# Tree attention on one core: TensorE one pair ahead at first, V copied in halves, loads reordered

## The chip, the core and the metric

The kernel runs on one core of a Trainium2 chip. A core has five engines with a queue of instructions each: TensorE (PE; its weight loads are listed as PEld), VectorE (DVE), ScalarE (ACT), GpSimd (POOL) and SyncE (SP), and 16 DMA engines that move data between the device's memory (HBM) and the core's SBUF. An engine works through its queue in order and waits where the next instruction waits. The metric is the device time of one execution in microseconds.

## The reference

Attention over 8 x 12 = 96 heads of 512 positions and 64 dimensions, in which position i may see only itself and its ancestors in a binary tree (the parent of i is (i-1)//2):

```python
    scores = np.einsum('bhqd,bhkd->bhqk', Q, K) * scale
    scores = scores + (1 - mask) * (-1e9)

    weights = np.exp(scores - np.max(scores, axis=-1, keepdims=True))
    weights = weights / (np.sum(weights, axis=-1, keepdims=True) + 1e-10)

    return np.einsum('bhqk,bhkd->bhqd', weights, V).astype(np.float32)
```

Inputs and output are float32.

## The kernel before

The 512 positions of a head lie in SBUF as 128 partitions of 4 "slots". Two heads make a pair; there are 48 pairs (`NP`), and 8 heads (four pairs) make a group (`GB`, 12 groups). The loop variable `i` of the main loop counts pairs. Pair i does the following:

- `transpose(i)` (L250): 16 small TensorE transpositions turn the pair's K and Q into keys and queries with the dimension on partitions. They land in the PSUM tile `kqp`, of which there is one. `evac(i)` (L276, VectorE) copies it to SBUF as `kq`.
- `scores1(i)` and `scores2(i)` (L287 to L325): matmuls that first add mask codes and then the products of keys and queries. The tree is split into an upper part that all queries see (scores1) and a lower part that is restricted to a few key blocks per query (scores2). ScalarE takes the exponential of each (L298, L321), into `e1` and `e2`.
- `values(i)` (L347): 20 matmuls of the exponentials with V, into the PSUM tile `ob`, of which there is one. A column of ones beside V gives the sums of the weights.
- `norm(i)` (L376, L377, VectorE): reciprocal of the sums and the multiplication, into `of`.

V doesn't arrive in the order in which `values` reads it. For each group it is copied from the load tile `vst` into the tile `vt`, in ten copies that all stand at L209: four "l7" copies (`spread_l7`, 32 partitions, VectorE), four "top" copies (`spread_top`, 32 partitions, mostly GpSimd) and two "leaf" copies (`spread_leaves`, 64 partitions, ScalarE or GpSimd). A whole group gives shapes of 32x1024, 32x512 and 64x1024; half a group (4 heads) gives 32x512, 32x256 and 64x512. `vt` has two buffers of two groups each. `spread(i)` says which copies are issued in iteration i. For i below 12 a table (`early_copies`) lists them; from 12 on it is a quarter of group i//4+1 in each iteration: an l7 copy, and on GpSimd two top copies or one leaf copy. Where an iteration has copies on both engines, `after()` makes the first GpSimd copy wait for the last VectorE copy.

All loads but those of the first pair, and all stores, are issued from GpSimd's queue (L189, L385), so they stand in one order with GpSimd's copies. Loads turn float32 into bf16 on the way. Each of K, Q and V has four load tiles of a group each. `loads_at(i)` says which loads are issued in iteration i: the start issues heads 0 to 15 in pieces of 4 heads, and from head 16 on each load is a whole group (8 heads). Stores begin in iteration 33, one group in each iteration; the last group is stored in three pieces.

The whole order on each engine is the order in which these functions are called (`manual_schedule`). In the main loop iteration i calls scores1(i), scores2(i), values(i-1), norm(i-1), transpose(i+2), evac(i+2), spread(i) and the loads or stores of i. Only iterations 1 to 3 differ, by this table:

```python
    AHEAD = {1: (2, 3), 2: (), 3: (4, 5)}
```

`fill(i, n)` issues n matmuls of zeros at the start, while there is no data.

Of the kernel before, what the change touches and what calls it, by code (L numbers as in the profile page):

```python
# [98 lines left out]
def kernel(  # L99
# [12 lines left out]
    NH = B * H  # L112
    NP = NH // 2
# [100 lines left out]
    def spread_top(eng, j, g, h0=0, h1=GB):  # L214
        return copy(
            eng, vtile(g)[32 * j:32 * j + 32, h0:h1, 0, 0:D],
            vsts[g][0:32, h0:h1, UNITS[TOP + j][1], :],
        )

    def spread_leaves(eng, r, g, h0=0, h1=GB):  # L220

        p = 64 if r else 0
        return copy(
            eng, vtile(g)[p:p + 64, h0:h1, 1 + r:4 + r:2, 0:D],
            vsts[g][64:128, h0:h1, r:3 + r:2, :],
        )
# [27 lines left out]
    def transpose(i):  # L254
        kqp = psT.tile([P, 2, 32, 32], bf16, name="kqp")
        kqps[i] = kqp
        for t in range(4):
            for a in range(2):
                transpose_one(kqp[:, 0, :, :], i, a, t, _slot_layout(t)[1], ksts, perms[t])
        for x, t in enumerate(ORDER):  # L260
            for a in range(2):
                transpose_one(
                    kqp[:, 1, :, :], i, a, t, [2 * x, 2 * x + 1, 2 * x + 9, 2 * x + 10],
                    qsts, qperm,
                )

    def evac(i):
        kq = work.tile([P, 2, 16, 32], bf16, name="kq")
        kTs[i] = kq[:, 0, :, :]
        qTs[i] = kq[:, 1, :, :].rearrange("p (t u) c -> p t (u c)", t=4)  # L270
        src = kqps[i][:, :, 0:18, :]
        src = bass.AP(
            src.tensor, src.offset,
            [list(src.ap[0]), [1024, 2], [32, 8], [9 * 32, 2], [1, 32]],
        )
        nc.vector.tensor_copy(  # L276
            out=kq[:, :, :, :].rearrange("p k (x y) c -> p k x y c", y=2), in_=src
        )
# [48 lines left out]
    def fill(i, n):  # L327

        if i not in obs:
            obs[i] = psO.tile([P, 2, 512], fp32, name="ob")  # L330
        for k in range(n):
            nc.tensor.matmul(
                out=obs[i][:, k % 2, :], lhsT=zeros[:, 0:128], rhs=zeros[:, :],
                start=True, stop=True,
            )

    def values(i):

        if i == NP - 1:
            obs[i] = psT.tile([P, 2, 512], fp32, name="kqp")  # L340
        elif i not in obs:
            obs[i] = psO.tile([P, 2, 512], fp32, name="ob")
        ob = obs[i]
        e1, e2, vt = ets[i], e2s[i % NE], vtile(2 * i // GB)

        def product(e, a, t, tile_v, lo=0, hi=128, **flags):
            nc.tensor.matmul(  # L347
                out=ob[lo:hi, a, 65 * t:65 * t + 65],
                lhsT=e[:, a, PLACE[t], lo:hi],
                rhs=vt[:, 2 * i % GB + a, tile_v, 0:D + 1],  # L350
                **flags,
            )

        def first(a):
            for t in range(4):
                product(e1, a, t, 0, start=t == 0, stop=False)
            for t in (2, 3):
                product(e2, a, t, 1 + t, start=False, stop=False)

        def second(a):  # L360
            for t in (0, 1):
                product(e2, a, t, 1 + SELF[t], 0, 64, start=False, stop=t == 1)
                product(e2, a, t, 1 + t, 64, 128, start=False, stop=t == 1)

        order = (first, second) * 2 if i == NP - 1 else (first, first, second, second)
        for n, part in enumerate(order):
            part(n // 2 if i == NP - 1 else n % 2)

    def norm(i, heads=((0, 2),)):
        g, r = divmod(i, 4)  # L370
        if r == 0:
            ofs[g] = opool.tile([P, GB, 4, D], fp32, name="of")
        for a0, a1 in heads:
            o4 = obs[i][:, a0:a1, 0:260].rearrange("p a (t c) -> p a t c", c=D + 1)
            rec = small.tile([P, a1 - a0, 4, 1], fp32, name="rec")
            nc.vector.reciprocal(out=rec[:, :, :, :], in_=o4[:, :, :, D:D + 1])  # L376
            nc.vector.tensor_tensor(  # L377
                out=ofs[g][:, 2 * r + a0:2 * r + a1, :, :],
                in0=o4[:, :, :, 0:D],
                in1=rec[:, :, :, :].to_broadcast([P, a1 - a0, 4, D]),  # L380
                op=ALU.mult,
            )
# [13 lines left out]

    DVE, ACT, POOL = nc.vector, nc.scalar, nc.gpsimd

    def early_copies(i):

        def l7(g, js, *h):
            return [(spread_l7, DVE, j, g) + h for j in js]

        def top(g, js, *h):
            return [(spread_top, POOL, j, g) + h for j in js]

        def leaf(eng, g, rs, *h):
            return [(spread_leaves, eng, r, g) + h for r in rs]

        every = range(4)  # L410
        return {
            0: l7(0, every, 0, 4) + [(spread_top, DVE, j, 0, 0, 4) for j in every]
            + leaf(ACT, 0, (0, 1), 0, 4),
            1: l7(0, every, 4, 8) + top(0, every, 4, 8) + leaf(ACT, 0, (0, 1), 4, 8),
            3: l7(1, every, 0, 4) + top(1, every, 0, 4) + leaf(ACT, 1, (0, 1), 0, 4),
            5: l7(1, every, 4, 8) + top(1, every, 4, 8) + leaf(ACT, 1, (0, 1), 4, 8),
            6: l7(2, (0,)) + top(2, (0, 1)) + leaf(ACT, 2, (0,)),
            7: l7(2, (1, 2)) + top(2, (2, 3)) + leaf(ACT, 2, (1,)),
            8: l7(2, (3,)),
            9: l7(3, (0,)) + top(3, (0, 1)),  # L420
            10: l7(3, (1, 2)) + top(3, (2, 3)) + leaf(ACT, 3, (1,)),
            11: l7(3, (3,)) + leaf(POOL, 3, (0,)),
        }.get(i, [])

    def spread(i):

        g, j = i // 4 + 1, i % 4
        if i < 12:
            todo = early_copies(i)
        elif g < NG:  # L430
            todo = [(spread_l7, DVE, j, g)]
            if j < 2:
                todo += [(spread_top, POOL, k, g) for k in (2 * j, 2 * j + 1)]
            else:
                todo += [(spread_leaves, POOL, j - 2, g)]
        else:
            todo = []
        last = None
        for f, eng, *args in todo:
            done = f(eng, *args)  # L440
            if eng is DVE:
                last = done
            elif eng is POOL and i >= 6 and last is not None:
                after(done, last)
                last = None

    def loads_at(i):

        k4 = lambda h: [(load_k, h, 4), (load_q, h, 4)]
        start = [(load_v, 0, 4), (load_k, 2, 2), (load_q, 2, 2)] + k4(4) + [(load_v, 4, 4)]  # L450
        start += k4(8) + [(load_v, 8, 4)] + k4(12)
        early = {
            -1: start, 1: [(load_v, 12, 4), (load_v, 16), (load_k, 16)], 2: [(load_q, 16)],
            3: [(load_v, 24), (load_k, 24)],
            5: [(load_q, 24), (load_v, 32), (load_k, 32), (load_q, 32)],
            9: [(load_v, 40)], 10: [(load_k, 40)],
            11: [(load_q, 40), (load_v, 48)], 12: [(load_k, 48), (load_q, 48)],
        }
        if i in early:
            return early[i]  # L460
        g, j = i // 4 + 3, i % 4
        if i < 13:
            return []
        if j == 0:
            return [(load_q, GB * g)] if g < NG else []
        if j < 3 and g + 1 < NG:
            return [((load_v, load_k)[j - 1], GB * (g + 1))]
        return []

    stored = []  # L470

    def pool(i):
        for f, *args in loads_at(i):
            f(*args)
        if i >= 33:
            for g in range(len(stored), min((i - 4) // 4, NG - 2) + 1):
                if len(stored) < i - 32:
                    stored.append(g)
                    store(g)

    AHEAD = {1: (2, 3), 2: (), 3: (4, 5)}

    pool(-1)
    fill(0, 8)
# [2 lines left out]
    evac(0)  # L487
    scores1(0)
    scores2(0)
    fill(0, 5)  # L490
    transpose(1)
    spread(0)
    evac(1)
    values(0)
    norm(0)
    for i in range(1, NP + 1):
        if i < NP:
            scores1(i)
            scores2(i)
        if i >= 2:  # L500
            values(i - 1)
            norm(i - 1, ((0, 1), (1, 2)) if i == NP else ((0, 2),))
        for n in AHEAD.get(i, (i + 2,)):
            if n < NP:
                transpose(n)
                evac(n)
        spread(i)
        pool(i)
        if i == NP - 2:
            store(NG - 1, 0, 4)  # L510
# [32 lines left out]
```

## Time and profile before

| | |
|---|---|
| median of 3 runs | 138.09 us (137.7 to 138.58) |
| the profiled execution | 137.91 us, its span 136.2 us |
| mean granted TensorE clock | 0.964 |
| HBM read, written | 38.01 MB, 12.58 MB |
| busy: PE, DVE, ACT, POOL | 116.5, 102.8, 92.5, 93.1 us |
| instructions | 5474 |

Times inside the profile count from the start of the span. A line of the timeline gives start, duration, engine, source line, operation, output and inputs with shapes, and in brackets how long the engine had been idle and what ended that. In the lists of 40 digits each digit is one slice of 3.4 us, in tenths busy; PEclk is the TensorE clock that was granted, in tenths of full speed; GB/s counts the bytes written.

### The profile page before, as it was taken

How to read it: one execution, taken by the hardware profiler on the slowest of the kernel's cores; microseconds unless marked ns; L12 is line 12 of the kernel's file. 1: busy time of each engine (PE TensorE's matmuls, PEld its weight loads, DVE VectorE, ACT ScalarE, POOL GpSimd, SP SyncE). 2: the span in 40 equal slices, each digit the busy share in tenths (PEclk: the TensorE clock that was granted, in tenths of full speed). 3: DMA queues.
4: the chain of work that ended last, by engine and by line, in shares of the span. 5: the costliest groups of instructions: out<-in, count | busy, mean ns of one | idle time of the engine just before them, and what ended most of it. 6: DMA issues, size and time to landing. Idle time of an engine off the chain costs nothing.

```text
span 136.2 us, 5474 instructions
## 1 busy us (share of the span) xinstructions
PE 116.5 (86%) x2413; PEld 81.0 (60%) x2413; DVE 102.8 (75%) x215; ACT 92.5 (68%) x110; POOL 93.1 (68%) x129
## 2 busy tenths in 40 slices
PE   6899859989898997999999798989989499979900
PEld 2336546757576775777676576767667376757500
DVE  2485766698799999899879777988989567785530
ACT  4174983799989777578686586868686456757700
POOL 6973999703356999786996776767888755781240
PEclk9999995999999999999999999999999959999995
DMA  4999999999999999999999999999999999999971
GB/s 115 226 189 195 197 196 198 199 197 199 202 194 200 197 200 197 198 197 198 197 199 200 195 199 197 198 198 198 202 306 406 401 402 394 402 390 398 375 303 48
DMA packets 41082, 32.34 MB, mean 238 GB/s; under 512 B 954, under 2 KB 37946, under 8 KB 41058
## 3 DMA queue, kind: packets, MB, share of 16 engines
q0 software_dynamic: 40320, 31.20, 125.2%
q1 hardware_dynamic: 466, 0.53, 1.2%
q8 instruction: 19, 0.31, 0.8%
q10 hardware_dynamic: 272, 0.26, 0.6%
q14 instruction: 5, 0.04, 0.1%
HBM read 38.01 MB, written 12.58 MB: 372 GB/s over the span
## 4 chain that ended last, share of the span: by engine, by line
PE 47%; DMA 15%; POOL 14%; issue 12%; DVE 5%; ACT 3%; POOLq 1%; ACTq 0%
PE ob L347 16%; PE kqp L250 10%; DMA qst<-in_Q_dram 9%; PE s L287 7%; DMA vst<-in_V_dram 5%; PE s L316 5%; PE s L292 5%; PE s L310 5%; POOL vt L209 5%; POOL vst L189 3%; POOL qst L189 2%; POOL kst L189 2%; DVE vt L209 2%; POOL out_dram L385 2%; DVE of L377 2%
## 5 line engine op out<-in xcount | busy, mean ns | idle before, releaser
L298 ACT ACTIVATE e<-s 128x1024 bf16<-128x1024 f32 x48 | 49.2, 1024 | 32.9 <-PE s L292 32.5
L209 POOL COPY vt<-vst 32x512 bf16<-32x512 bf16 (+2 forms) x69 | 46.7, 676 | 30.8 <-DVE vt L209 24.0
L347 PE MATMUL ob<-vt,e 128*128 128x65 bf16 (+1 forms) x940 | 38.3, 198 | 2.6 <-DVE of L377 1.2
L321 ACT ACTIVATE e<-s 128x768 bf16<-128x768 f32 x48 | 38.6, 805 | 0.1
L276 DVE COPY kq<-kqp 128x1024 bf16<-128x1024 bf16 x48 | 32.8, 683 | 6.2 <-PE kqp L250 6.1
L347 PEld LDWEIGHTS <-e 128*128 128x128 bf16 (+1 forms) x960 | 31.0, 103 | 10.8 <-issue 1.8
L377 DVE TENSOR_TENSOR of<-ob,rec 128x512 f32<-128x512 f32 x47 | 32.5, 691 | 1.6
L209 DVE COPY vt<-vst 32x1024 bf16<-32x1024 bf16 (+2 forms) x60 | 28.2, 470 | 1.7 <-DMA vst<-in_V_dram 0.2
L250 PE MATMUL kqp<-ptile,kst 128*64 128x128 bf16 x384 | 20.1, 225 | 4.9 <-issue 2.6
L250 PE MATMUL kqp<-ptile,qst 128*64 128x128 bf16 x384 | 19.9, 225 | 1.4 <-issue 1.0
L316 PEld LDWEIGHTS <-kq 64*128 64x128 bf16 x384 | 14.9, 96 | 9.5 <-issue 2.7
L287 PE MATMUL s<-ctile 40*128 40x512 bf16 x96 | 19.4, 399 | 0.8 <-ACT e L298 0.7
L376 DVE RECIPROCAL rec<-ob 128x8 f32<-128x8 f32 x47 | 9.7, 207 | 13.8 <-PE ob L347 12.0
L292 PE MATMUL s<-kq 64*128 64x512 bf16 x96 | 19.0, 390 | 0.6 <-issue 0.4
L316 PE MATMUL s<-kq 64*128 64x64 bf16 (+1 forms) x384 | 18.4, 213 | 0.7 <-issue 0.7
L310 PE MATMUL s<-ctile 40*128 40x480 bf16 x96 | 18.3, 377 | 0.5
L250 PEld LDWEIGHTS <-kst 128*64 128x64 bf16 x384 | 13.5, 113 | 7.1 <-issue 6.1
L385 POOL DMA_DIRECT2D out_dram<-of x14 | 12.0, 854 | 6.6 <-DVE of L377 6.6
L250 PEld LDWEIGHTS <-qst 128*64 128x64 bf16 x384 | 14.4, 114 | 1.7 <-issue 1.1
L189 POOL DMA_DIRECT2D vst<-in_V_dram x14 | 12.1, 865 | 0.9 <-POOLq L527 0.8
L310 PEld LDWEIGHTS <-ctile 40*128 40x128 bf16 x96 | 7.3, 97 | 8.7 <-issue 2.5
L189 POOL DMA_DIRECT2D qst<-in_Q_dram x14 | 12.2, 872 | 0.0
(22 smaller groups left out, 44.3 us busy)
## 6 DMA issues: line engine op xcount, KB each, us to landing
out_dram<-of POOLq DMA_DIRECT2D x11, 1024.0 KB, 9.5
vst<-in_V_dram POOLq DMA_DIRECT2D x10, 512.0 KB, 12.3
kst<-in_K_dram POOLq DMA_DIRECT2D x10, 512.0 KB, 12.9
qst<-in_Q_dram POOLq DMA_DIRECT2D x10, 512.0 KB, 12.4
vst<-in_V_dram POOLq DMA_DIRECT2D x4, 256.0 KB, 7.2
kst<-in_K_dram POOLq DMA_DIRECT2D x3, 256.0 KB, 8.0
qst<-in_Q_dram POOLq DMA_DIRECT2D x3, 256.0 KB, 8.6
out_dram<-of POOLq DMA_DIRECT2D x1, 512.0 KB, 6.0
```

The source lines that it names most:

```text
L189: nc.gpsimd.dma_start(out=kept[g][:, h0 % GB:h0 % GB + n, :, :].rearrange("p h t d -> p h (t d)"), in_=src[:, h0:h0 + n, :],)
L209: return (eng.copy if eng is nc.scalar else eng.tensor_copy)(out=out, in_=in_)
L250: nc.tensor.transpose(out=dst, in_=st[2 * i // GB][:, 2 * i % GB + a, t, :], identity=perm)
L276: nc.vector.tensor_copy(out=kq[:, :, :, :].rearrange("p k (x y) c -> p k x y c", y=2), in_=src)
L287: nc.tensor.matmul(out=sp[:, a, :], lhsT=k1code[64 * a:64 * a + BITS, :], rhs=q1code[64 * a:64 * a + BITS, :], start=True, stop=False,)
L292: nc.tensor.matmul(out=sp[:, a, :], lhsT=keys(i, a, TOP), rhs=qTs[i][64 * a:64 * a + 64, :, :].rearrange("p t c -> p (t c)"), start=False, ...
L298: nc.scalar.activation(out=et[:, :, :, :].rearrange("p a t c -> p (a t c)"), in_=sp[:, :, :].rearrange("p a c -> p (a c)"), func=AF.Exp, s ...
L310: nc.tensor.matmul(out=flat[:, a, 32:512], lhsT=k2code[64 * a:64 * a + BITS, :], rhs=q2code[64 * a:64 * a + BITS, 32:512], start=True, sto ...
L316: nc.tensor.matmul(out=flat[:, a, lo:hi], lhsT=keys(i, a, TILE2[t]), rhs=qTs[i][64 * a:64 * a + 64, :, :].rearrange("p t c -> p (t c)")[:, ...
L321: nc.scalar.activation(out=e2s[i % NE][:, :, :, 32:128].rearrange("p a t c -> p (a t) c"), in_=sp[:, :, :, 32:128].rearrange("p a t c -> p ...
L347: nc.tensor.matmul(out=ob[lo:hi, a, 65 * t:65 * t + 65], lhsT=e[:, a, PLACE[t], lo:hi], rhs=vt[:, 2 * i % GB + a, tile_v, 0:D + 1], **flags,)
L377: nc.vector.tensor_tensor(out=ofs[g][:, 2 * r + a0:2 * r + a1, :, :], in0=o4[:, :, :, 0:D], in1=rec[:, :, :, :].to_broadcast([P, a1 - a0, ...
```

## The change

Three things change, and the arithmetic stays the same.

1. Order on TensorE. Up to iteration 9 (`TURN`), transpose(i+1) stands ahead of values(i-1); from iteration 9 on, transpose(i+2) stands behind values(i-1), as before. Iteration 9 does both. The start (pairs 0 and 1) is written out anew, with 2 instead of 5 further matmuls of zeros.
2. Copies of V. Heads 4 to 31 are copied in halves of a group. Each half h from 2 on (heads 4h to 4h+3) is spread over the two iterations 2h-1 and 2h: two l7 copies, two top copies and a leaf copy in each, the leaf copy on ScalarE in the first and on GpSimd in the second. Before, groups 0 and 1 were copied by halves in one iteration each, and groups 2 and 3 whole. From group 4 on, `spread(i)` takes a quarter of group (i-1)//4+1 instead of i//4+1. `after()` holds from group 4 on.
3. Loads. The start issues 12 loads from GpSimd instead of 11. K and Q of heads 16 to 39 and V of heads 24 to 31 come in pieces of 4 heads, in an order of their own; from head 40 on the order is K, Q, V of each group, and from iteration 13 on each iteration issues one load.

```diff
-    def early_copies(i):
...
+    EARLY = 4
+
+    def halves(i):
+
+        def part(h, l7, top, acts, pools):
+            g, h0 = h // 2, 4 * (h % 2)
+            return (
+                [(spread_l7, DVE, j, g, h0, h0 + 4) for j in l7]
+                + [(spread_top, POOL, j, g, h0, h0 + 4) for j in top]
+                + [(spread_leaves, ACT, r, g, h0, h0 + 4) for r in acts]
+                + [(spread_leaves, POOL, r, g, h0, h0 + 4) for r in pools]
+            )
+
+        if i == 2:
+            return part(1, range(4), (), (), ())
+        h = (i + 1) // 2
+        if i < 3 or h >= 2 * EARLY:
+            return []
+        return part(h, (0, 1), (0, 1), (0,), ()) if i % 2 else part(h, (2, 3), (2, 3), (), (1,))
 
     def spread(i):
 
-        g, j = i // 4 + 1, i % 4
-        if i < 12:
-            todo = early_copies(i)
-        elif g < NG:
-            todo = [(spread_l7, DVE, j, g)]
+        g, j = (i - 1) // 4 + 1, (i - 1) % 4
+        todo = halves(i)
+        if EARLY <= g < NG:
+            todo += [(spread_l7, DVE, j, g)]
             if j < 2:
                 todo += [(spread_top, POOL, k, g) for k in (2 * j, 2 * j + 1)]
             else:
                 todo += [(spread_leaves, POOL, j - 2, g)]
...
-            elif eng is POOL and i >= 6 and last is not None:
+            elif eng is POOL and g >= EARLY and last is not None:
...
-    def loads_at(i):
...
+    def plan():
 
         k4 = lambda h: [(load_k, h, 4), (load_q, h, 4)]
...
+        seq = [(load_v, 0, 4), (load_k, 2, 2), (load_q, 2, 2)]
+        for h in (4, 8, 12):
+            seq += k4(h) + [(load_v, h, 4)]
+        seq += k4(16) + [(load_v, 16)] + k4(20) + [(load_v, 24, 4)] + k4(24) + [(load_v, 28, 4)]
+        seq += k4(28) + k4(32) + [(load_v, 32)] + k4(36)
+        for h in range(40, NH, GB):
+            seq += [(load_k, h), (load_q, h), (load_v, h)]
+        counts = {-1: 12, 1: 2, 3: 1, 4: 2, 5: 1, 6: 2, 7: 1, 8: 2, 9: 1, 10: 2, 11: 1, 12: 2}
+        at = {}
+        for i in range(-1, 33):
+            n = counts.get(i, 1 if i > 12 else 0)
+            at[i], seq = seq[:n], seq[n:]
...
-    AHEAD = {1: (2, 3), 2: (), 3: (4, 5)}
+    def ready(n):
+        if n < NP:
+            transpose(n)
+            evac(n)
+
+    def finish(i):
+        values(i)
+        norm(i, ((0, 1), (1, 2)) if i == NP - 1 else ((0, 2),))
+
+    TURN = 9
...
-    fill(0, 5)
+    for r in range(2):
+        spread_leaves(ACT, r, 0, 0, 4)
     transpose(1)
-    spread(0)
+    for j in range(4):
+        spread_top(DVE, j, 0, 0, 4)
     evac(1)
-    values(0)
-    norm(0)
-    for i in range(1, NP + 1):
+    fill(0, 2)
+    for j in range(4):
+        spread_l7(DVE, j, 0, 0, 4)
+    scores1(1)
+    scores2(1)
+    finish(0)
+    for j in range(4):
+        spread_top(POOL, j, 0, 4, 8)
+    spread_leaves(ACT, 0, 0, 4, 8)
+    spread_leaves(POOL, 1, 0, 4, 8)
+    ready(2)
+    finish(1)
+    pool(1)
+    for i in range(2, NP + 1):
         if i < NP:
             scores1(i)
             scores2(i)
-        if i >= 2:
-            values(i - 1)
-            norm(i - 1, ((0, 1), (1, 2)) if i == NP else ((0, 2),))
-        for n in AHEAD.get(i, (i + 2,)):
-            if n < NP:
-                transpose(n)
-                evac(n)
+        if i <= TURN:
+            ready(i + 1)
+        if i > 2:
+            finish(i - 1)
+        if i >= TURN:
+            ready(i + 2)
         spread(i)
         pool(i)
```

More of the change, by code (lines that the diff above doesn't have):

```diff
@@ L397 @@
     DVE, ACT, POOL = nc.vector, nc.scalar, nc.gpsimd
-    def early_copies(i):
[L401 to L423, printed above, removed]
-    def spread(i):
-        g, j = i // 4 + 1, i % 4
-        if i < 12:
-            todo = early_copies(i)
-        elif g < NG:
-            todo = [(spread_l7, DVE, j, g)]
+    EARLY = 4
[14 more added lines that the diff above has]
+        return part(h, (0, 1), (0, 1), (0,), ()) if i % 2 else part(h, (2, 3), (2, 3), (), (1,))
+    def spread(i):
+        g, j = (i - 1) // 4 + 1, (i - 1) % 4
+        todo = halves(i)
+        if EARLY <= g < NG:
+            todo += [(spread_l7, DVE, j, g)]
             if j < 2:
@@ L435, in spread @@
                 todo += [(spread_leaves, POOL, j - 2, g)]
-        else:
-            todo = []
         last = None
@@ L442, in spread @@
                 last = done
-            elif eng is POOL and i >= 6 and last is not None:
+            elif eng is POOL and g >= EARLY and last is not None:
                 after(done, last)
                 last = None
-    def loads_at(i):
+    def plan():
         k4 = lambda h: [(load_k, h, 4), (load_q, h, 4)]
[L450 to L468, printed above, removed]
+        seq = [(load_v, 0, 4), (load_k, 2, 2), (load_q, 2, 2)]
[10 more added lines that the diff above has]
+            at[i], seq = seq[:n], seq[n:]
+        assert not seq
+        return at
+    LOADS = plan()
     stored = []
     def pool(i):
-        for f, *args in loads_at(i):
+        for f, *args in LOADS.get(i, ()):
             f(*args)
```

## The prediction

> **What bounds the kernel now.** I read the page's busy shares and its 40 slices first.
>
> ```profile
> PE 116.5 (86%) x2413; PEld 81.0 (60%) x2413; DVE 102.8 (75%) x215; ACT 92.5 (68%) x110; POOL 93.1 (68%) x129
> ...
> PE   6899859989898997999999798989989499979900
> ...
> PEclk9999995999999999999999999999999959999995
> DMA  4999999999999999999999999999999999999971
> GB/s 115 226 189 195 197 196 198 199 197 199 202 194 200 197 200 197 198 197 198 197 199 200 195 199 197 198 198 198 202 306 406 401 402 394 402 390 398 375 303 48
> ```
>
> Two things run nearly all the time. The DMA engines are 99% busy from the second slice: loads to about 100 us, then stores. TensorE is at 8 to 9 tenths, and its clock halves in two slices. Which of them sets the end shows in the timeline of the last microseconds: the last store is issued as soon as the last division is done, and the span ends 5.1 us later.
>
> ```profile
> 131.07 0.72 POOL L385 DMA_DIRECT2D out_dram<-of  x1 [0.92 <-DVE of L377]
> ```
>
> So a later last pair moves the end one for one, while an earlier one gains little: the last two slices move 303 and 48 GB/s x 3.4 us = 1.2 MB, 3.0 us of full-rate work, so the store queue would empty only some 1.3 us earlier.
>
> Next the timeline of two ordinary pairs. TensorE repeats every 2.11 us: values of pair 18 at 59.09, of pair 19 at 61.20.
>
> ```profile
> 59.09 0.79 PE L347 MATMUL ob<-vt,e 128*128 128x65 bf16 x20
> 59.38 0.76 DVE L209 COPY vt<-vst 32x1024 bf16<-32x1024 bf16 x1
> ...
> 60.17 0.21 DVE L376 RECIPROCAL rec<-ob 128x8 f32<-128x8 f32 x1
> ...
> 61.02 0.68 DVE L276 COPY kq<-kqp 128x1024 bf16<-128x1024 bf16 x1
> ...
> 61.20 0.79 PE L347 MATMUL ob<-vt,e 128*128 128x65 bf16 x20
> ...
> 61.73 0.61 DVE L209 COPY vt<-vst 32x1024 bf16<-32x1024 bf16 x1
> ...
> 62.48 1.04 POOL L209 COPY vt<-vst 64x1024 bf16<-64x1024 bf16 x1 [0.36 <-DVE vt L209]
> ...
> 63.46 0.53 PE L347 MATMUL ob<-vt,e 128*128 128x65 bf16 x12
> ```
>
> The copies at 61.73 and 62.48 are the last of group 5 (spread(19)). Pair 20, the first of group 5, starts its values at 63.46 where 63.31 was due: these copies end just as they are needed, 63.52. That is the row on which the prediction turns.
>
> Beyond that TensorE loses time in gaps put down to "issue" (0.31, 0.96, 0.35, 0.45, 0.29, 0.46, 1.77, 0.27, 0.88 after 56 us, 5.7 in all), about every 6 us. The longest is followed by a slow stretch. Timeline, then busy time by stretch (length, PE, PEld, DVE, ACT, POOL, granted clock, DMA, GB/s):
>
> ```profile
> 106.18 0.22 PE L250 MATMUL kqp<-ptile,kst 128*64 128x128 bf16 x1
> ...
> 108.17 0.41 PE L250 MATMUL kqp<-ptile,kst 128*64 128x128 bf16 x7 [1.77 <-issue]
> ```
>
> ```profile
> 17.09:20.50 3.41, 1.79 (x46) 1.40 (x46) 2.38 (x5) 2.83 (x4) 3.19 (x7) 1.00 1.45 196
> 20.50:23.92 3.42, 3.35 (x42) 2.22 (x41) 2.19 (x6) 1.22 (x2) 3.14 (x7) 0.50 1.45 197
> 75.10:78.51 3.41, 2.45 (x62) 1.73 (x58) 2.53 (x5) 1.87 (x3) 2.48 (x5) 1.00 1.46 197
> 105.83:109.24 3.41, 1.64 (x39) 1.12 (x37) 2.00 (x4) 1.22 (x2) 2.34 (x3) 1.00 1.02 401
> 109.24:112.66 3.42, 3.42 (x52) 2.39 (x50) 2.07 (x5) 1.73 (x2) 1.87 (x2) 0.50 1.02 399
> ```
>
> A 3.4 us stretch with 1.64 or 1.79 us of matmul was followed by 3.42 us at half clock; one with 2.45 was not. The later dip cost 1.47 us (scores at 108.73, 112.00, 114.42: 3.27 + 2.42 against 2 x 2.11).
>
> **Late part: spread one iteration later (groups 4 to 11).** Before, `spread(i)` takes group i//4+1; after, (i-1)//4+1. So the last quarter of group g, an l7 copy on VectorE and behind it the 64x1024 leaf copy on GpSimd, moves from iteration 4g-1 to 4g. Pair 4g is the group's first, and its values stand in iteration 4g+1, two stages on from the values of pair 4g-1. In iteration 4g VectorE must first divide pair 4g-1, copy out a transposition, then do l7; GpSimd waits for l7 (`after`). Durations from the timeline: values' start to reciprocal 0.83 (56.98 to 57.81), to multiply 0.25, to the copy-out 0.60, to l7 0.72, l7 0.61, hand-over 0.14, leaf copy 1.04: 4.19 us. Due are 2.11 us plus the 0.19 us of five matmuls that need no leaf. TensorE stands for 4.19 - 2.30 = 1.9 us, once a group. Bounds: 1.5 if l7 takes 0.42 and the rest runs closer; 2.13 by the rows above as they lie (59.09 to 63.52 is 4.43). Behind the waiting matmul stand all later transpositions and scores, so ScalarE and VectorE wait too, and nothing gives it back: TensorE at 2.11 a pair is the pace. Seven stalls after the one of pair 16: +13.3 us (10.5 to 14.9).
>
> Longer groups hide the "issue" gaps. They come every 6.3 us (70.3 to 121.0 in eight steps), a group now takes 10, so some 63% of the intervals hold a stall that is longer than nearly every gap; and loads that run with less backlog should shorten the rest. I take -4.5 of 5.7 (0 to -5.7), and -0.9 for the dip behind the 1.77 gap (63% of 1.47).
>
> **Clock.** A 1.9 us stall wholly within a 3.41 us stretch leaves 1.5 us of matmul, as little as the two stretches that were followed by a dip. By position that is (3.41 - 1.9)/3.41 = 44%, 3 or 4 of 8 stalls; I take 3 x 1.47 = +4.4 (0 to +11.7), as a group of 4 x 2.11 + 1.9 = 10.3 us is close to three stretches and the positions will hardly change from group to group.
>
> The Trainium skill, "TensorE: Matmul & The Clock Gate", Part 1, has the clock fall after an idle window of about 3.4 us, free-running. The trace agrees on the length (3.42 us) but not on the condition: the dip at 109.24 followed a stretch half busy. By the page the clock term would be nothing; that is a rival below.
>
> **Early part: transposition one pair ahead, V by halves, loads reordered.** Loads land in order of issue at about 0.333 us a head (131 KB at twice 197 GB/s, bf16 written from fp32) plus 4.4 to 5.3. The chain has both checks: 24 head-loads by 12.44, 72 by 29.23.
>
> ```profile
> 5.02 7.42 DMA vst<-in_V_dram
> ...
> 16.65 12.58 DMA qst<-in_Q_dram
> ```
>
> The second is a wait: pair 8 needed all of heads 16 to 23. Now K and Q of heads 16 to 19 are the 56th (23.7 us), so that wait goes; so do the two transpositions in a row of iteration 3, with the 1.2 us wait at 19.4 and the dip behind it. What is late next is GpSimd. For two pairs it does four 32x256 copies (1.69), a leaf copy of 512 elements (0.61, by the 32x512 row) and three issues (3 x 0.87): 4.9 us. (In all GpSimd gets seven more load issues, 49 for 42, 6.1 us, and 4.8 us more of copies, 51.5 for 46.7, nearly all before pair 16.) VectorE needs 0.90 + 0.68 + 2 x 0.40 = 2.4 a pair, the same pace. From V of heads 8 to 11 landing at 17.0, the leaf copies end at 20.2 for pair 4, then every 4.9: 39.8 for pair 12 (before: values of pair 12 at 45.03). Iterations 13 and 14 copy heads 28 to 31 and group 4 at once: 45.97 for pair 14 (before 49.39), and pair 16, with its own stall (48.1 + 4.19), resumes at 52.3 instead of 55.04. I take -2.7 (+1 to -8.2; the far end if neither copy engine is the pace and pairs follow at 2.11 from pair 4). The fill's 3 x 0.44 us fewer, and 2.5 us of ScalarE copies fewer (9 x 0.61 for 8 x 0.61 + 3 x 1.04), lie beside waits for the transposition's copy-out and cost or bring nothing; without that cover the fills would be 1.3 us of gain.
>
> Later loads go one per iteration, K, Q, V. A group takes 8.0 us of DMA against 10 of computing, so they keep up; their queue is short, and so is the last store's: -0.3.
>
> **Sum.** -2.7 + 13.3 - 4.5 - 0.9 + 4.4 - 0.3 = +9.3 on the profiled execution's 137.91 (span 136.2 and 1.7 around it): 147.2; the median of the runs stood 0.2 above that execution: 147.4 us.
>
> **Rivals.** *Stalls, but no dip of the clock*: gaps of 0.96 and 0.88 left none, and 1.9 split over two stretches is as mild; against it are the two dips. 147.4 - 4.4 = 143.0. This is what the skill's page would give. *A dip behind every stall*: five more, +7.3: 154.7; the two stretches speak for it, the need to lie in one stretch against. *Loads late*: if V of a group lands 12.3 us after issue, as the page's median had it, three iterations (7.8 us) after its issue VectorE stands 4.5 us in l7, once, since later groups gain on it: 151.9; against it, that median is a queue of large loads issued far ahead. *Early lead wins*: copies in halves keep out of TensorE's way and pairs run at 2.11 from pair 4: a lead of 8.2 at pair 16. It decides if the stalls stay at 1.5 or less with no dip: -8.2 + 10.5 - 4.5 - 0.9 = -3.1, of which the store queue leaves 1.3: 136.8, faster. For it is that the early waits do go; against it GpSimd's 4.9 us. *Nothing to be measured*: early gain, hidden gaps and stalls cancel, or the late copies have slack that one group's rows don't show: 138.
>
> **Chances.** Forecast 0.46 (own range 144.5 to 150.5), no dip 0.20, every dip 0.13, loads late 0.09, cancelling 0.06, early lead 0.06. The range reaches over no dip and most of the way to every dip, 141.5 to 154. Faster by over 1%: 0.06; within 1% (about what a measurement of this kernel can tell from no change): 0.06; slower by over 1%: 0.88.
>
> **What would show it.** Right: values of pairs 16, 20, ... 44 broken after a few matmuls, TensorE waiting for GpSimd's vt copy about 1.9 us eight times; pair 16 resuming near 52; short issue gaps; two to four slices of lower clock; the last store issued near 140. Wrong: no TensorE wait for GpSimd after 55 us, or waits below 1 us; values of pair 12 still at 45 (no early gain) or before 36; DMA shares well under 9 before 90 us.

## The result and the profile after

The changed kernel took 151.88 us (median of 4 runs, 149.95 to 154.36) against 138.34 before: a ratio of 1.094, 95% interval 1.082 to 1.106. Some executions of one kernel take a few per cent longer than the rest; medians in this document are of all runs, ratios leave those longer runs out. The profiled execution took 149.95 us with a span of 148.2, that is 12.0 more than the profiled execution before. The slices of the page:

```profile
PE   6888899999787396994995995995995994986930
...
PEclk9999999999999869999999999699999999998685
DMA  4999999999999599999999999999999999998551
GB/s 138 217 191 200 193 199 195 197 195 197 198 194 127 63 147 182 166 132 171 158 192 183 195 197 197 198 198 183 182 287 408 398 398 406 396 396 338 231 216 74
```

From the nineteenth slice on TensorE's busy share has a hole in every third slice (a slice is 3.7 us). DMA, full before, falls to 63 GB/s near 48 us and stays short of 197 until 80. At the end the stores no longer fill the engines (231, 216, 74): the last ones wait for computing. The last is issued at 144.06 instead of 131.07, and the span ends 4.14 us later instead of 5.13:

```profile
144.06 0.72 POOL L385 DMA_DIRECT2D out_dram<-of  x1 [1.16 <-DVE of L377]
```

One hole in the timeline, at pairs 19 and 20, the first of group 5:

```profile
64.45 0.79 PE L347 MATMUL ob<-vt,e 128*128 128x65 bf16 x20
...
64.89 0.79 DVE L209 COPY vt<-vst 32x1024 bf16<-32x1024 bf16 x1
...
65.71 0.21 DVE L376 RECIPROCAL rec<-ob 128x8 f32<-128x8 f32 x1
...
66.56 0.68 DVE L276 COPY kq<-kqp 128x1024 bf16<-128x1024 bf16 x1
66.79 0.28 PE L347 MATMUL ob<-vt,e 128*128 128x65 bf16 x4 [0.16 <-DVE of L377]
...
67.25 0.64 DVE L209 COPY vt<-vst 32x1024 bf16<-32x1024 bf16 x1
67.95 0.20 PE L347 MATMUL ob<-vt,e 128*128 128x65 bf16 x1 [0.88 <-DVE vt L209]
68.02 1.03 POOL L209 COPY vt<-vst 64x1024 bf16<-64x1024 bf16 x1 [0.36 <-DVE vt L209]
...
69.11 0.62 PE L347 MATMUL ob<-vt,e 128*128 128x65 bf16 x15 [0.96 <-POOL vt L209]
```

Pair 20 begins its values, does four matmuls, waits 0.88 us for the l7 copy, does one, and waits 0.96 us for the leaf copy. From scores to scores this pair takes 4.50 us instead of 2.11. The same stands at pairs 24, 28, ... 44.

### The profile page after: what moved, and what is told of

Same layout as the page of the kernel before. It is cut to its first block, busy times and chain, and to the rows that moved or that the text cites. A ratio compares the mean times of both kernels' runs of the same rounds, so it can differ in the third digit from the quotient of the medians.

```text
span 148.2 us, 5496 instructions
## 1 busy us (share of the span) xinstructions
PE 118.1 (80%) x2410; PEld 82.2 (55%) x2410; DVE 106.1 (72%) x223; ACT 89.7 (61%) x108; POOL 101.3 (68%) x150
## 4 chain that ended last, share of the span: by engine, by line
PE 35%; DVE 31%; POOL 15%; issue 12%; DMA 4%; POOLq 1%
PE ob L347 14%; DVE vt L209 10%; DVE of L377 9%; POOL vt L209 9%; DVE kq L276 9%; PE kqp L250 8%; PE s L287 4%; DMA qst<-in_Q_dram 4%; PE s L292 3%; PE s L310 3%; DVE rec L376 3%; PE s L316 3%; POOL qst L189 2%; POOL out_dram L385 2%; POOL kst L189 2%
## 5 line engine op out<-in xcount | busy, mean ns | idle before, releaser
L209 POOL COPY vt<-vst 32x512 bf16<-32x512 bf16 (+3 forms) x83 | 51.4, 619 | 35.0 <-DVE vt L209 28.2
L347 PE MATMUL ob<-vt,e 128*128 128x65 bf16 (+1 forms) x940 | 42.0, 200 | 20.9 <-POOL vt L209 11.1
L347 PEld LDWEIGHTS <-e 128*128 128x128 bf16 (+1 forms) x960 | 32.6, 104 | 31.7 <-issue 14.3
L321 ACT ACTIVATE e<-s 128x768 bf16<-128x768 f32 x48 | 38.7, 805 | 0.0
L209 DVE COPY vt<-vst 32x512 bf16<-32x512 bf16 (+2 forms) x68 | 31.5, 463 | 1.9 <-DMA vst<-in_V_dram 0.3
L250 PE MATMUL kqp<-ptile,kst 128*64 128x128 bf16 x384 | 19.6, 226 | 0.6 <-DMA ptile<-tree_perms 0.3
L316 PE MATMUL s<-kq 64*128 64x64 bf16 (+1 forms) x384 | 17.9, 213 | 0.0
L250 PEld LDWEIGHTS <-kst 128*64 128x64 bf16 x384 | 13.0, 113 | 2.3 <-DVE kst L204 0.8
L189 POOL DMA_DIRECT2D kst<-in_K_dram x17 | 13.8, 814 | 0.0
L189 POOL DMA_DIRECT2D qst<-in_Q_dram x17 | 13.8, 812 | 0.0
L189 POOL DMA_DIRECT2D vst<-in_V_dram x15 | 12.7, 844 | 1.5 <-POOLq L536 0.8
```

The source lines that it names most:

```text
L189: nc.gpsimd.dma_start(out=kept[g][:, h0 % GB:h0 % GB + n, :, :].rearrange("p h t d -> p h (t d)"), in_=src[:, h0:h0 + n, :],)
L209: return (eng.copy if eng is nc.scalar else eng.tensor_copy)(out=out, in_=in_)
L250: nc.tensor.transpose(out=dst, in_=st[2 * i // GB][:, 2 * i % GB + a, t, :], identity=perm)
L316: nc.tensor.matmul(out=flat[:, a, lo:hi], lhsT=keys(i, a, TILE2[t]), rhs=qTs[i][64 * a:64 * a + 64, :, :].rearrange("p t c -> p (t c)")[:, ...
L321: nc.scalar.activation(out=e2s[i % NE][:, :, :, 32:128].rearrange("p a t c -> p (a t) c"), in_=sp[:, :, :, 32:128].rearrange("p a t c -> p ...
L347: nc.tensor.matmul(out=ob[lo:hi, a, 65 * t:65 * t + 65], lhsT=e[:, a, PLACE[t], lo:hi], rhs=vt[:, 2 * i % GB + a, tile_v, 0:D + 1], **flags,)
```

## The experiments

Each ratio is to the kernel before on the same chip. Where there is none, the lowest and the highest run stand in its place.

| kernel | median us | ratio, 95% interval |
|---|---|---|
| late_alone | 147.67 | 1.057 (1.045 to 1.070) |
| leaf_early | 147.31 | 1.061 (1.049 to 1.072) |
| pileup_freed | 150.44 | 1.085 (1.075 to 1.095) |
| late_undone | 151.69 | none (149.36 to 153.42 us) |
| loads_alone | 148.91 | 1.074 (1.066 to 1.082) |
| undone_freed | 149.35 | 1.077 (1.067 to 1.086) |
| undone_loads_ahead | 140.34 | 1.005 (0.9997 to 1.010) |
| stall_filled | 149.79 | none (147.36 to 151.61 us) |
| loads_ahead_only | 151.73 | 1.091 (1.082 to 1.101) |
| late_and_loads | 153.58 | 1.098 (1.090 to 1.107) |
| early_spread | 140.86 | 1.008 (1.003 to 1.014) |
| after_again | 151.89 | 1.085 (1.077 to 1.094) |

**late_alone.** The kernel before, with only the quarters of groups 4 to 11 one iteration later:

```diff
-        g, j = i // 4 + 1, i % 4
-        if i < 12:
+        g, j = (i - 1) // 4 + 1, (i - 1) % 4
+        if i <= 12:
```

> The kernel before with one edit: from group 4 on, the quarter of a group is copied one iteration later. Theory 1 (the late copies are the loss): TensorE stands 2.3 us before the values of pairs 16, 20, ... 44 (8 x 2.3 = 18), the 8.9 us that the kernel before loses after pair 18 beyond 2.11 us a pair go nearly all, one or two dips of the clock come (+2): 148 to 151 us. Theory 2 (the early part loses): within 1% of the kernel before, 137 to 139.5.

147.67 us. Every group's first pair stands as in the changed kernel. TensorE's waits (line waited for: us in total, times, longest):

```profile
PE ob L347 <- POOL vt L209: 7.7, 8, 1.0
PE ob L347 <- DVE vt L209: 5.1, 8, 0.9
```

There are eight waits for the leaf copy and eight for l7, with 4.0 to 4.6 us from scores to scores at each. Theory 1 had the mechanism, with a range that began 0.3 us too high; the early part isn't needed for a loss of 6%. No gap put down to "issue" of 0.25 us or more is left on TensorE after 56 us here either, and the DMA engines stay full to about 87 us: these gaps vanish with the stalls, and emptier DMA queues aren't needed for it.

**leaf_early.** The changed kernel, with the second leaf copy issued with the first, an iteration earlier:

```diff
-            else:
-                todo += [(spread_leaves, POOL, j - 2, g)]
+            elif j == 2:
+                todo += [(spread_leaves, POOL, r, g) for r in range(2)]
```

> The changed kernel with the second leaf copy of groups 4 to 11 on GpSimd one iteration earlier, so that of the late quarter only VectorE's l7 copy is left. Theory (the stall is a chain of division, copy-out, l7 and leaf copy): each stall falls from 2.3 to 1.1 us, the l7 part; 7 or 8 x 1.2 = 8 to 10 us shorter, less what comes back of the issue gaps (up to 3): 143 to 146 us. Rival (only the leaf copy matters, or only l7): stalls of 0.3 or less (139 to 141), or unchanged (150 to 152).

147.31, 4.6 less than the changed kernel but 1.3 above the expectation. The wait for the leaf copy goes. The one for l7 grows: l7 now runs beside GpSimd's copies and takes 0.97 us instead of 0.64 (the l7 copy at 69.86, with GpSimd standing idle, takes 0.42):

```profile
67.59 0.67 PE L347 MATMUL ob<-vt,e 128*128 128x65 bf16 x16 [1.21 <-DVE vt L209]
```

A group's first pair takes 3.72 instead of 4.50: a stall of 1.6 us is left, where 1.1 was expected. So the stall is a chain, as the prediction had it, and both copies are links of it.

**pileup_freed.** The second cause I looked for was the early part. Pair 12 had come 2.8 us sooner than before (scores at 38.91 against 41.71), but pair 16 resumed its values, after the wait for its own leaf copy, 3.2 us later (58.28 against 55.04). GpSimd stands 5.5 us for VectorE's l7 copy of iteration 13, and then TensorE 3.0 us for GpSimd at the values of pair 14 (timeline of the changed kernel):

```profile
45.89 2.36 POOL L209 COPY vt<-vst 32x256 bf16<-32x256 bf16 x4 [5.52 <-DVE vt L209]
...
50.17 0.31 PE L347 MATMUL ob<-vt,e 128*128 128x65 bf16 x5 [3.03 <-POOL vt L209]
```

The edit takes that wait away:

```diff
-            elif eng is POOL and g >= EARLY and last is not None:
+            elif eng is POOL and i > 14 and last is not None:
```

> The changed kernel, but in iterations 13 and 14 GpSimd's copies don't wait for VectorE's. Theory: the 3.4 us that TensorE stood at the values of pair 14 came from GpSimd standing 5.5 us for VectorE's l7 copy of iteration 13, with the copies of two groups behind it: pair 16 resumes at 54 to 55 instead of 58.3, the slices of DMA at 63 and 127 GB/s are gone, and the run is 3 to 4 us shorter than the changed kernel (146 to 148.5). Rival: the copies of both groups are simply too much work for those two iterations: pair 16 resumes within 1 us of 58.3, 150 to 152.

150.44: the rival. GpSimd waits no more at iteration 13, but pair 14 now waits for VectorE (1.29 and 0.82 us), whose three l7 copies there take 2.21 us; GpSimd's own wait for VectorE comes back at iteration 15 (4.60 us); and from the scores of pair 3 to the resuming of pair 16 it is 42.35 us against 42.94. The copies of two groups in iterations 13 and 14 are what is late, on whichever engine (early_spread below moves them apart).

**late_undone.** The changed kernel with the quarters back in their old iterations:

```diff
-        g, j = (i - 1) // 4 + 1, (i - 1) % 4
+        g, j = i // 4 + 1, i % 4
```

> The changed kernel with the quarters of groups 4 to 11 back in the iteration in which the kernel before had them; halves, order and loads stay changed. Theory 1: no waits of 2 us at pairs 20 to 44, the issue gaps are back: 137 to 140 us, with the store queue's end at 136.6 as the floor. Theory 2: the wait at pair 14 and the dry DMA queue near 45 to 50 us stay and cost 3 us or more against the kernel before: 141 to 145.

151.69 beside 151.88: no gain that shows, and both theories missed. The holes behind the late copies are gone, but VectorE now waits for V itself, and the DMA engines are dry earlier and longer (timeline, then the slices):

```profile
72.00 0.41 DVE L209 COPY vt<-vst 32x1024 bf16<-32x1024 bf16 x1 [3.68 <-DMA vst<-in_V_dram]
```

```profile
GB/s 126 225 190 195 197 199 196 198 196 197 197 106 39 170 140 164 132 109 175 167 178 145 195 196 198 199 197 198 198 198 328 403 400 405 399 406 395 401 341 23
```

Here the stores do fill the engines to the end (395, 401, 341). A second loss seems to lie under the first; the next run asks whether it is the loads.

**loads_alone.** The kernel before, with only the loads from head 40 on as in the changed kernel (before, V of head 40 was issued in iteration 9 and K in 10):

```diff
-            9: [(load_v, 40)], 10: [(load_k, 40)],
...
+        n = i - 12
+        if 0 <= n < 21:
+            return [((load_k, load_q, load_v)[n % 3], 40 + GB * (n // 3))]
```

> The kernel before with one edit: from head 40 on the loads go K, Q, V and one in each iteration from iteration 12, as in the changed kernel (there from 12 too). Theory (in the changed kernel V of a group is issued too close to its copies, which the late copies cover): VectorE waits for V at the first copies of groups 5 and 6 (iterations 16 and 20), 1 to 4 us each: 140 to 144. Rival (loads never matter): 137 to 139.5.

148.91, 5 us beyond the theory's range. Between the last early load and the first late one GpSimd issues nothing for 21 us:

```profile
25.92 0.90 POOL L189 DMA_DIRECT2D qst<-in_Q_dram  x1
...
47.34 0.88 POOL L189 DMA_DIRECT2D kst<-in_K_dram  x1
```

and VectorE then stands 10.1 us in all for V, 5.11 of it at the first copy of group 5. The expectation counted only such waits. It left out that the DMA engines are at work from start to end before, so a microsecond that they stand dry (with no load to work on) is added to the end: slices of 20, 88, 194, 166, 130 and 112 GB/s follow 44 us. The edit tests late loads as such, not the changed kernel's own, which issues smaller loads up to iteration 12 and has no gap as long.

I worked out the dry time of each profile: for every slice from the third to the last before the stores, the part by which it falls short of 197 GB/s, times the slice.

| profile | span us | dry | span less dry | last store issued | from there to the end |
|---|---|---|---|---|---|
| before | 136.2 | 0.3 | 135.9 | 131.1 | 5.1 |
| loads_alone | 147.0 | 11.5 | 135.5 | 135.1 | 11.9 |
| late_undone | 148.4 | 12.4 | 136.0 | 138.6 | 9.8 |
| undone_freed | 147.6 | 11.5 | 136.1 | 137.0 | 10.6 |
| leaf_early | 144.6 | 8.1 | 136.5 | 135.8 | 8.8 |
| early_spread | 137.9 | 2.3 | 135.6 | 129.2 | 8.7 |
| undone_loads_ahead | 138.8 | 1.7 | 137.1 | 132.6 | 6.2 |
| the changed kernel | 148.2 | 9.3 | 138.9 | 144.1 | 4.1 |
| late_and_loads | 149.9 | 10.2 | 139.7 | 146.0 | 3.9 |
| loads_ahead_only | 149.3 | 7.8 | 141.5 | 145.2 | 4.1 |
| pileup_freed | 149.1 | 10.9 | 138.2 | 144.9 | 4.2 |
| late_alone | 146.4 | 3.9 | 142.5 | 142.5 | 3.9 |
| stall_filled | 146.1 | 9.1 | 137.0 | 142.0 | 4.1 |
| after_again | 151.1 | 9.6 | 141.5 | 147.0 | 4.1 |

The last column tells the two bounds apart. In the last seven rows, all kernels with both late copies (l7 and leaf), the end follows the last store by 3.9 to 4.2 us: computing ends last. In the first seven rows the last store waits in a queue, 5.1 to 11.9 us to the end, and the end is the DMA engines' work, 136 to 137 us, plus the time that they were dry. early_spread shows it best: it issues its last store 1.9 us before the kernel before does, and ends 1.7 us after it. leaf_early crossed from one bound to the other: its last store is issued 8.3 us earlier than the changed kernel's, but its span is only 3.6 us shorter.

**undone_freed.** late_undone and pileup_freed together:

> The changed kernel with the quarters of groups 4 to 11 back in their old iterations and GpSimd not waiting for VectorE in iterations 12 to 14; loads as in the changed kernel. If the wait of 4.8 us on GpSimd's queue is what let the DMA engines run dry and V of groups 5 and 6 come late: VectorE's waits for V fall from 6.4 us to under 3 and the run takes 142 to 147. If the loads' own order is enough to be late: as with the quarters put back alone, 149 to 153.

149.35: the second case. VectorE still waits 6.3 us for V, and the dry time is 11.5. GpSimd's waits for VectorE in these iterations are not what makes the loads late. GpSimd now stands 3.6 us for V itself in iteration 12. The next run changes the loads' order and dates.

**undone_loads_ahead.** As undone_freed, with the loads ahead:

```diff
-            seq += [(load_k, h), (load_q, h), (load_v, h)]
-        counts = {-1: 12, 1: 2, 3: 1, 4: 2, 5: 1, 6: 2, 7: 1, 8: 2, 9: 1, 10: 2, 11: 1, 12: 2}
+            seq += [(load_v, h), (load_k, h), (load_q, h)]
+        counts = {-1: 12, 1: 2, 3: 1, 4: 2, 5: 1, 6: 2, 7: 1, 8: 2, 9: 1, 10: 2, 11: 3, 12: 3}
```

> As the kernel with the quarters back and GpSimd free in iterations 12 to 14, and besides from head 40 on V ahead of K and Q, three loads in iterations 11 and 12. Theory (early order and halves are worth something when neither the late quarters nor late loads take it back): no wait for V, no wait of 2 us before values, pair 16 resumes near 52 to 54, and the end is set by the store queue: 136.5 to 139.5. Rival (halves and the pile-up with group 4 cost by themselves): pair 16 at 57 or later, 140 to 145.

140.34, ratio 1.005: within 1% of the kernel before. With late copies and late loads both undone, the rest of the change (order of transpositions, halves, small loads) brings and costs nothing that shows. Pair 14 still waits 3.2 us for GpSimd, and pair 16 starts its values at 58.5, so the rival had the pile-up right. The median lies at the foot of its range too; but the kernel before took 139.06 on that chip, so the pile-up costs some 1% at most where the DMA engines set the end.

**loads_ahead_only.** The changed kernel with the loads ahead and the late copies kept (as above, with no load in iteration 20, where V would otherwise wait for copies behind it):

> The changed kernel with its late copies and its waits of iterations 13 and 14, but from head 40 on V ahead of K and Q and three loads each in iterations 11 and 12. Theory (two bounds, of which the later counts: the DMA engines' work of 136 us plus the time that they stand dry, and the chain of late copies): the dry time falls from 9.3 us to under 4, the chain of late copies is left and now sets the end: 146 to 149, 2 to 5 us less than the changed kernel. Rival (losses add up): the 9 us come back whole, 141 to 143. Rival (dry time doesn't matter): 150 to 153.

151.73, beside 151.89 for the changed kernel on the same chip (after_again). The number is that of the rival without an effect of dry time, but the run doesn't test that: the dry time fell by 1.5 us only, not below 4. Loads are issued iteration by iteration, and iterations still go at the pace of the late copies, so the engines run dry later instead, between 70 and 107 us. TensorE's wait is the old one:

```profile
PE ob L347 <- POOL vt L209: 11.1, 10, 3.0
```

**late_and_loads.** The kernel before with both edits and its own early part:

> The kernel before with both edits, the late copies and the late order of loads, but its own early part. Theory of two bounds: 149 to 152, at most 3 us above the slower of the two alone (147.7 and 148.9), near the changed kernel. Rival (losses add up): 139 + 8.6 + 9.9 = 157.

153.58, above the range by 1.6 and 4.7 above the slower single edit, but far from 157. As ratios: 1.057 and 1.074 alone, 1.098 together, where a sum would be 1.131. The two losses overlap; and this is as slow as the changed kernel without anything of its early part.

**after_again.** The changed kernel once more, on the chip of loads_ahead_only, late_and_loads and early_spread:

> The changed kernel as it is, for a comparison on the same chip and with the same runs of the kernel before: 149.5 to 152.5, 8 to 10% above it, the DMA engines' GB/s under 180 in several slices between 44 and 80 us.

151.89, ratio 1.085, within the interval of the result (1.082 to 1.106).

**early_spread.** As undone_loads_ahead, with the halves of heads 24 to 31 an iteration earlier:

> As the kernel with the quarters back and the loads ahead, and the halves of heads 24 to 31 copied one iteration earlier, so that less falls on iterations 13 and 14. Theory: the wait of 3.2 us at pair 14 and the slow clock behind it shrink, pair 16 resumes at 53 or earlier; the DMA work is the floor, so no more than 1% is to be gained on the kernel before: 136.8 to 139. Rival (the pile-up just moves): as the kernel without it, 139 to 141.

140.86, in the rival's range, ratio 1.008. Pair 16 starts its scores at 50.44 instead of 53.55 and resumes its values at 55.14, later than the 53 expected; computing ends sooner, but the time doesn't follow: the dry time is 2.3 us and the floor is the DMA work. No version here beats the kernel before.

**stall_filled.** The changed kernel with matmuls in the holes:

```diff
     def finish(i):
+        if i >= 16 and i % 4 == 0:
+            fill(i, 6)
         values(i)
```

> The changed kernel with six matmuls of zeros ahead of the values of pairs 16, 20, ... 44, into the accumulator that these values then overwrite. They stand where TensorE would wait (six of 0.22 us are 1.3 us in a wait of 2.3), so the wait itself is as long as before. Theory (after some of the waits the clock halves for 3.4 us, at 1 to 1.5 us each): no dip behind a late-copy stall, mean clock 0.97 or more after pair 20, and 2 to 4 us shorter than the changed kernel: 148 to 150. Rival (the dips come from elsewhere, or cost nothing since TensorE then waits less): 150.5 to 153.

The profile has no dip behind a late copy (the granted clock in 40 slices; the one dip, near 52 us, is behind pair 14's wait), and from the scores of pair 17 to those of pair 47 it is 81.4 us against 83.3:

```profile
PEclk9999999999999968999999999999999999999997
```

That is about the 2 us that two dips (slices of half clock) cost there in the changed kernel's profile. The median of 149.79 lies in the theory's range, but of four runs two took 148.0 and 147.4 and two 151.6, so the gain in time is not shown.

## Why the prediction was right, and where it wasn't

It forecast 147.4 us, slower, from the late copies; it was 151.88, slower, outside its forecast's own range (144.5 to 150.5) but inside the wide one. The late copies alone give 1.057 of the 1.094. By its own terms, against the 12.0 us between the two profiled executions:

| term | predicted | measured |
|---|---|---|
| early part, to pair 16's resuming | -2.7 | +3.2 |
| seven stalls, pairs 20 to 44 | +13.3 | +16.0 |
| issue gaps and the old dip go | -5.4 | -8.9 |
| new dips of the clock | +4.4 | +2.1 |
| tail | -0.3 | -1.0 |
| not assigned | | +0.6 |

That the sum came within 2.7 us of the 12.0 is in part luck: the early part was missed by 5.9 us and the stalls by 2.7, and the gaps and dips took back 5.8.

*Stalls.* Right in place and mechanism. The size is 2.3 us each (2.39, 2.28, 2.38, 1.85, 2.43, 2.42, 2.28 over 2.11), not 1.9: VectorE starts its division 1.26 us after the values begin (64.45 to 65.71) instead of 0.83, because l7 of the iteration before still runs. The prediction had that in its upper bound, 2.13, and chose the prompt rows; the chain as it lay in the trace was the better price.

*Gaps.* Stalls of 2.3 us hid all "issue" gaps, not 63% of them: after 56 us none of 0.25 us is left, and the whole 8.9 us by which the kernel before exceeded 2.11 us a pair from pair 18 on is gone.

*Clock.* Two dips behind late copies in this profile where three were taken; a third, near 51 us behind the wait of pair 14, is part of the early part's row. The term varies from run to run: another run, with a mean clock of 0.924 instead of 0.948, took 2.2 us more of span (150.4). But a run at 0.946 took 1.6 us more as well (149.8), so the clock is not all that varies. The rival without dips (143.0) fell. What decides is how a stall lies on a grid of 3.41 us (see the last section). The Trainium skill, "TensorE: Matmul & The Clock Gate", Part 1, asks for an idle window; the windows ahead of these two dips were about half busy (1.56 and 1.65 us of 3.41), so here the measurement decides.

*Early part.* This step failed. GpSimd's pace was about right up to pair 12: it took 4.6 to 4.7 us for two pairs, not 4.9, and ended the leaf copies for pair 12 at 38.7, not 39.8. But the pair's values began at 41.96 and stood until 42.99 for VectorE's l7 copy, so GpSimd was not the pace there, and the lead over the kernel before (45.03) was 3.1 us at most, not 5.2. Then the sum took iterations 13 and 14 as more work on a queue that never waits. There `after()` made GpSimd wait 5.5 us for VectorE, and pair 14, forecast for 45.97, stood until 50.17. pileup_freed shows that the wait is only one form of it: the copies of two groups fall together.

*Loads.* "They keep up" was wrong: the engines stood dry for 9.3 us, which the prediction had named as a sign against itself. It compared rates, 8.0 us of loads against 10 of computing, and not the backlog: up to iteration 12 the kernel before has issued K, Q and V of heads 0 to 55, the changed one K of heads 0 to 47 and Q and V of heads 0 to 39. That is 40 loads of a head fewer, by the prediction's 0.333 us some 13 us of work for the DMA engines (an estimate). Its rival of late loads looked for waits on VectorE, and in the changed kernel there are almost none (0.3 us in all), since late copies ask late. So the error hardly showed in the time: in the changed kernel computing ends last. It shows once the late copies go: late_undone is no faster. The prediction took the DMA engines as a bound at the very end only, and did not ask what their standing dry would cost.

What stays open is how the loss beyond the late copies' own 5.7% divides. With late copies, the early pile-up brings it to 1.091 with the loads issued ahead (loads_ahead_only, where computing ends last), and late loads bring it to 1.098 without the pile-up (late_and_loads). How much each of the two gives in the changed kernel itself is not shown.

## What to carry to other kernels

When two resources are both busy to the end, two faults can each cost most of the loss, and undoing one brings little: test each alone on the good kernel as well as undone on the bad one. Look in the trace for the copy that ends just when its reader starts; moving it by one stage costs the length of its chain less the time until its reader is due, each time. And where a DMA queue is full from start to end, count its dry time in the middle of a run as time at its end; whether it or computing ends last shows in the time from the last store's issue to the end.

## What the runs showed of the hardware

The clock's grid. The dips in both profiles fit one rule: time falls into stretches of 3.41 us that don't shift at a stall, and after a stretch with too little matmul the next is at half clock. In the changed kernel (length, PE, PEld, DVE, ACT, POOL, clock, DMA, GB/s):

```profile
47.48:50.89 3.41, 0.36 (x7) 0.26 (x7) 1.88 (x4) 1.09 (x2) 3.15 (x7) 1.00 0.24 20
50.89:54.31 3.42, 3.42 (x48) 2.19 (x48) 1.93 (x4) 0.71 (x1) 2.52 (x4) 0.51 1.17 151
...
78.20:81.61 3.41, 1.87 (x40) 1.29 (x42) 1.49 (x4) 0.78 (x2) 2.14 (x3) 1.00 1.38 182
88.44:91.85 3.41, 1.56 (x38) 1.21 (x40) 1.48 (x4) 1.27 (x2) 2.74 (x4) 1.00 1.45 197
91.85:95.27 3.42, 3.42 (x50) 2.39 (x50) 2.11 (x5) 1.73 (x2) 1.74 (x3) 0.51 1.46 199
...
132.81:136.22 3.41, 1.65 (x38) 1.26 (x40) 1.46 (x4) 1.29 (x2) 2.06 (x3) 1.00 0.90 351
136.22:139.64 3.42, 3.42 (x40) 1.96 (x38) 1.79 (x4) 1.73 (x2) 0.00 (x0) 0.51 0.84 335
```

The grid drawn from the dip at 91.85 also gives the one before it (12 x 3.413 earlier, 50.89) and the one behind it (13 x 3.413 later, 136.22). Stretches with 0.36, 1.56 and 1.65 us of matmul were followed by a dip, as were 1.64 and 1.79 in the kernel before; 1.87 was not, nor were stalls that the grid cuts in two (2.37 and 2.45 us on either side of 67.96). The edge is known only roughly. The granted 0.51 instead of 0.50 (2% of a stretch still at full clock) says that the grid lies some 0.07 us later than drawn, and there the 1.87 reads 1.95. In two other profiles stretches of 2.00 us (late_alone) and 1.99 us (late_and_loads) were followed by a dip, and ones of 2.08 and 2.01 were not. So the edge lies near 2 us of 3.41, by busy time as the profile counts it.

The sum of two bounds. Span less dry time was 135.5 to 137.1 us in the seven profiles in which the last store waited in the queue, with spans from 136.2 to 148.4. In the seven in which it didn't, it was 137.0 to 142.5.

VectorE's copy beside GpSimd. The same 32x1024 copy took 0.42 us with GpSimd idle (leaf_early at 69.86), 0.64 and 0.79 beside GpSimd's issue of a load (the changed kernel at 67.25 and 64.89) and 0.97 beside GpSimd's own copies (leaf_early at 66.56). Why is not shown.
